# Q, K and V projections in pairs by way of DRAM, and attention woven from three streams

## The chip, the cores and the metric

The kernel runs on one core of a Trainium2 chip. Its time is the device time of one execution in microseconds (us). TensorE (PE) multiplies matrices, VectorE (DVE) and ScalarE (ACT) work elementwise, GpSimd (POOL) does small elementwise work and issues DMAs, SyncE (SP) issues most DMAs. Each engine runs its own instructions in a fixed order and waits for the others by semaphores.

## The reference

One decoder layer for a prompt of 512 tokens and 8 samples of 8 tokens each, 576 tokens in all (`T`), everything in float32. One combined projection of the normalised input (2048 wide) gives z, xBC, dt, q, k, v and three sets of gates; an SSD (scan) branch and a sliding-window attention branch follow, are gated, merged and projected out.

```python
h = _rmsnorm(x, norm_w)
u = jnp.einsum('bld,de->ble', h, w_in)
...
q, k, v, g_attn, mix_s, mix_a = ...        # columns of u; 32 query heads, 8 kv heads of 64
o = _banded_window_attention(q, k, v, rel_table, attn_sinks)   # prompt: window of 128
o = _window_decode_attention(q, kk, vv, rel_table, attn_sinks) # samples: cache of 128 + 8 new
...
s = q.k * scale + bias;  m = max(max(s), sink);  p = exp(s - m)
denom = sum(p) + exp(sink - m);  out = (p / denom) v
...
o = o * silu(g_attn);  p_attn = o @ w_attn_branch
merged = sigmoid(mix_s) * p_ssm + sigmoid(mix_a) * p_attn
x = x + merged @ w_out
```

Outputs are the two normalised results, the last keys and values, and the conv and scan states.

## The kernel before

*Products.* A product in float32 is made of three products of float32r parts: the weight tile (1024 x 128) is split into `wh` (ACT, L80) and `wl` (DVE, L81), the activations are kept as `ah` and `al`, and `wh.ah + wh.al + wl.ah` is summed in PSUM. `run_main` does this plainly: an output tile is 128 columns of the weights for all 576 tokens, as two halves of 288, so 16 row blocks x 2 halves x 3 = 96 matmuls of 288 columns (L345). `pairs_of` takes two output tiles, the two halves of the weight rows and the two halves of the tokens as a 2 x 2 block product and makes it with seven products instead of eight (L453, 7 x 8 x 3 = 168 matmuls); the price is sums of weight tiles on DVE (L393) and additions on the way out (L404).

*Stages.* In order of time: normalisation and the first `FIRST` = 6 mix gates, plainly; the **pair stage**, 22 pairs (16 tiles of the attention gate `ga` and `Z_PAIRED` = 28 tiles of z, stored to DRAM by ACT's DMA queue); the **attention stage**, `run_main` over 38 tiles (4 of K, 4 of V, dt, 16 of Q, 13 mix gates); the **scan stage**, `run_main` over 63 tiles (48 of xBC, 4 of z, 11 mix gates); then the output products, mostly in pairs, and the final normalisation.

*Weaving.* Other work is written as generators in two lists, `quick` and `jobs`. `run_main` calls `pump()` after every six matmuls; each call advances the head of `quick` by one step and `jobs` by `pace["rate"]`/8 steps. So the program's order puts attention and scan between the matmuls. From this order a scheduler makes each engine's list by a simulated timeline: work that would wait lets later work pass. What is wrapped in `keep_in_program_order` does not move on its engine.

*Attention.* `take_q` splits a Q tile straight from PSUM; when the fourth tile of a group of two kv heads is done, `attn_job(m)` is queued. For each of four blocks of 128 queries it makes the scores of 8 heads (L606), adds the bias and takes the maximum (L610), the exponential (L622), divides (L629), transposes (L639), copies (L641), multiplies by the values (L649, 512 columns) and copies into `oT` (L654). `sample_attn` does the same for the 8 samples; its last product is 16 matmuls of 64 columns (L742, L743). Then `oT` is multiplied by the gate on POOL (L665) and stored. The four groups run one after the other. The bias rows come from DRAM (`bias_d`), written during the pair stage by `bias_job` with 16 DMAs of POOL (L491).

*Gates.* A mix gate is a Sigmoid on ACT straight from PSUM (L1127), stored by SP. Where L1127 and the Exp of L622 alternate, the trace has an ACT_TABLE_LOAD ahead of each (11 and 10 of them in the attention stage).

Of the kernel before, what the change touches and what calls it, by code (L numbers as in the profile page):

```python
# [16 lines left out]
P = 128  # L17
D = 2048
# [26 lines left out]
N_A = 40  # L45
# [3 lines left out]
MIXES = (2, 2, 3, 6)  # L49
# [4 lines left out]
Z_PAIRED = 28  # L54
# [31 lines left out]
def hybrid(ctx, tc, x_prompt, x_sample, cache_k, cache_v, state_conv, state_ssm, norm_w, w_in, conv_w,  # L86
# [23 lines left out]

    def scratch(shape, name):
        return dram.tile(shape, F32, tag=name, name=name)
# [9 lines left out]
    ga_d = scratch([D, T], "ga_d")  # L122
    xb_d = scratch([D // 2, TH], "xb_d")
# [18 lines left out]
    eps = pers_tile([P, 1], "eps")  # L142
    sinkb = pers_tile([P, HEADS], "sinkb")
# [10 lines left out]
    vec.memset(eps, EPS)  # L154
    for hf in range(2):
        pl = slice(64 * hf, 64 * hf + 64)
        vec.tensor_copy(two[pl], ident[pl, pl])
# [110 lines left out]
    def open_pools(attention):  # L268
        stk = now["stack"] = ExitStack()
        if attention:  # L270
            cp = kp = stk.enter_context(tc.tile_pool(name="ap", bufs=N_A))
# [6 lines left out]
        now["c"], now["k"], now["kt"] = cp, kp, "c" if attention else "k"  # L278
# [4 lines left out]
    def kten(shape, name="k", dt=F32):  # L283
        return now["k"].tile(shape, dt, tag=now["kt"], name=name)
# [31 lines left out]
    def run_main(tiles, had=(), raws={}, then=None):  # L316
# [33 lines left out]

        n = 0
        while n < len(flat):
# [5 lines left out]
            for only in ((1,), (0,)) if had and n == 0 else ((0, 1),):  # L358
# [112 lines left out]
    def bias_job():  # L471

        rb, parts_ = ev.tile([P, TH], F32, tag="e", name="rb"), []
# [15 lines left out]
        for h in range(0, HEADS, 2):  # L489
            yield from wait(56)  # L490
            tc.keep_in_program_order(pool.dma_start(  # L491
# [3 lines left out]
    kT, vnat = [None] * 4, []  # L495

    def take_k(i):
        def f(ps):
            kT[i] = cten("kT")
            act.activation(sq(kT[i]), ps[:, :, :TH], AF.Copy)  # L500
            quick.append(knat_job(i))
        return f

    kn = {}

    def knat_job(i):
        yield
        if i == 0:
            kn["p"] = kten([P, 512], "knp")
            kn["s"] = kten([P, 512], "kns")  # L510
        p1 = bank()
        ten.transpose(p1[:, 0:P], kT[i][:, 384:512], ident)
        ten.transpose(p1[:NS, P:2 * P], kT[i][:, 512:T], ident)
        act.activation(kn["p"][:, i * P:(i + 1) * P], p1[:, 0:P], AF.Copy)
        act.activation(kn["s"][:NS, i * P:(i + 1) * P], p1[:NS, P:2 * P], AF.Copy)
        yield
        if i == 3:
            store_kv(k_prompt, k_sample, cache_k, kn["p"], kn["s"])
            yield

    def store_kv(out_p, out_s, cache, tp, ts):
        sync.dma_start(out=out_p[0, 0].rearrange("t h d -> t (h d)"), in_=tp)
        for b in range(NB):
            sync.dma_start(out=out_s[0, b, 120:128].rearrange("t h d -> t (h d)"), in_=ts[8 * b:8 * b + 8])
        quick.append(copy_job(out_s, cache))

    def copy_job(out_s, cache):
        for b in range(0, NB, 2):
            tc.keep_in_program_order(pool.dma_start(
                out=out_s[0, b:b + 2, 0:120].rearrange("b t h d -> b (t h d)"),  # L530
                in_=cache[0, b:b + 2, 8:128].rearrange("b t h d -> b (t h d)")))
            yield from wait(12)

    def take_v(i):
        def f(ps):
            vt = cten("vT")
            act.activation(sq(vt), ps[:, :, :TH], AF.Copy)
            quick.append(v_job(i, vt))
        return f

    def v_job(i, vt):
        yield
        if i == 0:
            vnat.extend(kten([P, 512], f"v{b}") for b in range(5))
        p1, p2 = bank(), bank()
        for b in range(4):
            ten.transpose(p1[:, b * P:(b + 1) * P], vt[:, b * P:(b + 1) * P], ident)
        ten.transpose(p2[:NS, :P], vt[:, 512:T], ident)
        for b in range(4):
            (act.activation(vnat[b][:, i * P:(i + 1) * P], p1[:, b * P:(b + 1) * P], AF.Copy) if b % 2 else  # L550
             vec.tensor_copy(vnat[b][:, i * P:(i + 1) * P], p1[:, b * P:(b + 1) * P]))
        act.activation(vnat[4][:NS, i * P:(i + 1) * P], p2[:NS, :P], AF.Copy)
        yield
        if i == 3:
            store_kv(v_prompt, v_sample, cache_v, vnat[3], vnat[4])
            yield

    qT, q_s = {}, {}

    def take_q(m, t):  # L560

        def f(ps):
            for u in range(2):
                qs = qT[m, 2 * t + u] = cten("qs", F32R)
                me, other = slice(64 * u, 64 * u + 64), slice(64 - 64 * u, 128 - 64 * u)
                act.activation(sq(qs)[me], ps[me, :, :TH], AF.Copy, scale=0.125)
                vec.scalar_tensor_tensor(out=sq(qs)[other], in0=ps[me, :, :TH], scalar=0.125, in1=sq(qs)[me],
                                         op0=ALU.mult, op1=ALU.subtract)
            q0 = q_s[m, t] = now["s"].tile([P, NS], F32, tag="qs", name="q0", bufs=8)
            act.activation(q0, ps[:, 1, 512 - TH:TH], AF.Copy, scale=0.125)  # L570
            if t == 3:
                jobs.append(attn_job(m))
        return f

    def attn_job(m):
        oT = [cten("oT") for _ in range(4)]
        bm = []
        for j in range(4):
            b_ = kten([P, 2, 256], "bm")
            sync.dma_start(out=b_, in_=AP(bias_d, (8 * m + 2 * j) * P * BL + 127, [[382, P], [P * BL, 2], [1, 256]]))  # L580
            bm.append(b_)

        ks = []
        for hf in range(2):
            kh, kl = (kten([P, 512], n, F32R) for n in ("kh", "kl"))
            src = kT[m][64 * hf:64 * hf + 64, :512]
            for d in (hf, 1 - hf):
                act.activation(kh[64 * d:64 * d + 64], src, AF.Copy)
            for d in range(2):
                vec.tensor_tensor(out=kl[64 * d:64 * d + 64], in0=src, in1=kh[64 * hf:64 * hf + 64],  # L590
                                  op=ALU.subtract)
            ks.append((kh, kl))
        yield from wait(4)

        def scores(blk):
            lo = 128 if blk == 0 else 0
            mx = stat(8, "mx")
            sc = []
            for j in range(4):
                ps = bank([P, 2, 256])  # L600
                s_ = kten([P, 2, 256], "sc")
                sc.append(s_)
                for i in range(2):
                    h = 2 * j + i
                    for d in range(2):
                        ten.matmul(ps[:, i, lo:256], qT[m, h][:, blk * P:(blk + 1) * P],  # L606
                                   ks[h // 4][d][:, blk * P - 128 + lo:blk * P + P], start=d == 0, stop=d == 1)
# [6 lines left out]
            nm, es, sm = stat(8, "nm"), stat(8, "es"), stat(8, "sm")  # L614
            sk_ = sinkb[:, 8 * m:8 * m + 8]
# [4 lines left out]
            for h in range(8):  # L620
# [3 lines left out]
            yield from wait(3)  # L624
            vec.tensor_tensor(out=sm, in0=sm, in1=es, op=ALU.add)
            vec.reciprocal(sm, sm)
            for h in range(8):
# [3 lines left out]
            yield from wait(6)  # L631
            pts = {}
            kbs = [1] if blk == 0 else [0, 1]
            for hf in range(2):
                for kb in kbs:
                    pt = bank()
                    for r in range(4):
                        j, i = divmod(4 * hf + r, 2)
                        ten.transpose(pt[:, r * P:(r + 1) * P], sc[j][:, i, kb * P:(kb + 1) * P], ident)  # L639
                    ptt = kten([P, 512], "pT")  # L640
                    act.activation(ptt, pt, AF.Copy)  # L641
                    pts[hf, kb] = ptt
                    yield
            yield from wait(2)
            po = bank()
            for kb in kbs:
                for hf in range(2):
                    col = (2 * m + hf) * 64
                    ten.matmul(po[64 * hf:64 * hf + 64, :], vnat[blk - 1 + kb][:, col:col + 64], pts[hf, kb],  # L649
                               start=kb == kbs[0], stop=kb == 1)  # L650
                yield
            for h in range(8):
                hf, r = divmod(h, 4)
                act.activation(oT[h // 2][64 * (h % 2):64 * (h % 2) + 64, blk * P:(blk + 1) * P],  # L654
# [895 lines left out]
```

## Time and profile before

| | |
|---|---|
| median of 3 runs | 3225.19 us (3222.79 to 3232.87) |
| profiled execution, own time | 3228.93 us |
| its span, first to last instruction | 3226.8 us |
| mean granted TensorE clock | 0.983 |
| busy: PE / DVE / ACT / POOL | 3112.4 / 1996.5 / 1473.7 / 482.5 us |
| HBM read / written | 385.79 / 91.81 MB |

In a row of the stage view stand the stretch (us from the span's start), its length, then for each engine its busy time and (x) the instructions in it, then the granted TensorE clock (1.00 is full), the mean busy share of the 16 DMA engines and GB/s. With one line chosen, only that line's matmuls and weight loads are counted. A row of the groups by line has the line, engine, operation, output <- inputs, shape and count, then busy time and mean ns of one, then idle time before them and who ended it. A row of the waits reads: who waited for whom, us in total, times, longest.

### The profile page before, as it was taken

Reading aid. Unit: us, or ns where it says so; the run is one execution under the profiler, and the core shown is the slowest. Engines: PE = TensorE matmul, PEld = TensorE weight load, DVE = VectorE, ACT = ScalarE, POOL = GpSimd, SP = SyncE. Lnnn points to the kernel's source line nnn. Section 1 sums busy time; section 2 is a strip of 40 time slices with the busy share of each in tenths; the row PEclk is TensorE's granted clock in tenths of the full one; section 3 lists DMA queues with packets and bytes.
Section 4 is the critical chain, followed back from the end, with each engine's and each line's share of the span. In section 5 each row is a group of like instructions: output and inputs, shape, how many; then the busy total and the mean of one; then the engine's idle time right before and its main releaser. Section 6 shows DMA issues by size and latency. Waiting matters only on the chain. (4 is left out here: it accounts for less than half of the span.)

```text
span 3226.8 us, 58215 instructions
## 1 busy us (share of the span) xinstructions
PE 3112.4 (96%) x22939; PEld 2993.4 (93%) x22939; DVE 1996.5 (62%) x3434; ACT 1473.7 (46%) x2761; POOL 482.5 (15%) x591
## 2 busy tenths in 40 slices
PE   6989999999999999999999999999999999999997
PEld 5989999999898998999999999998899989998997
DVE  6656666515444443477687687686657777877354
ACT  5434444423554554455555555565433433434333
POOL 3200000000001010112213212212221031311111
PEclk9999999999999999999999999999999999999999
DMA  6564444433343243364464564565575676967655
GB/s 198 143 156 121 122 123 125 117 89 90 84 121 93 82 123 100 100 165 135 135 179 128 147 166 132 148 166 146 147 234 175 194 212 143 249 159 194 180 161 158
DMA packets 733650, 471.18 MB, mean 146 GB/s; under 512 B 45433, under 2 KB 696969, under 8 KB 733185
## 3 DMA queue, kind: packets, MB, share of 16 engines
q1 hardware_dynamic: 691616, 420.51, 46.6%
q0 software_dynamic: 24336, 29.20, 4.4%
q10 hardware_dynamic: 17424, 17.76, 1.7%
q8 instruction: 180, 2.95, 0.4%
q14 instruction: 94, 0.76, 0.1%
HBM read 385.79 MB, written 91.81 MB: 148 GB/s over the span
## 5 line engine op out<-in xcount | busy, mean ns | idle before, releaser
L80 ACT ACTIVATE wh<-raw 128x1024 fp32r<-128x1024 f32 x586 | 620.1, 1058 | 1031.6 <-PE ps L453 488.4
L81 DVE TENSOR_TENSOR wl<-raw,wh 128x1024 fp32r<-128x1024 f32 x586 | 728.0, 1243 | 529.9 <-ACT wh L80 525.9
L345 PE MATMUL ps<-ah,wh 128*128 128x288 f32 (+2 forms) x4384 | 1021.4, 302 | 34.8 <-ACT craw L828 10.1
L345 PE MATMUL ps<-ah,wl 128*128 128x288 f32 (+2 forms) x4384 | 1012.6, 301 | 3.5 <-DVE wl L81 3.3
L345 PE MATMUL ps<-al,wh 128*128 128x288 f32 (+2 forms) x4384 | 1012.4, 300 | 2.5 <-DVE al L1170 2.5
L345 PEld LDWEIGHTS ps<-ah,wh 128*128 128x128 f32 x4384 | 735.2, 192 | 50.5 <-issue 11.1
L345 PEld LDWEIGHTS ps<-ah,wl 128*128 128x128 f32 x4384 | 734.5, 191 | 19.6 <-issue 10.6
L345 PEld LDWEIGHTS ps<-al,wh 128*128 128x128 f32 x4384 | 734.6, 191 | 9.0 <-DVE al L1170 4.1
L453 PE MATMUL ps<-ah,wh 128*128 128x288 f32 x1280 | 382.2, 299 | 13.8 <-DVE w L404 5.6
L453 PE MATMUL ps<-ah,wl 128*128 128x288 f32 x1280 | 383.5, 300 | 5.9 <-DVE wl L81 5.4
L453 PE MATMUL ps<-al,wh 128*128 128x288 f32 x1280 | 381.8, 298 | 0.0
L453 PEld LDWEIGHTS ps<-ah,wh 128*128 128x128 f32 x1280 | 244.4, 191 | 14.7 <-issue 5.8
L393 DVE TENSOR_TENSOR raw<-raw 128x1024 f32<-128x1024 f32 x160 | 194.8, 1220 | 97.6 <-DMA raw<-in_w_in_dram 40.6
L453 PEld LDWEIGHTS ps<-ah,wl 128*128 128x128 f32 x1280 | 244.6, 191 | 9.3 <-DVE wl L81 9.2
L453 PEld LDWEIGHTS ps<-al,wh 128*128 128x128 f32 x1280 | 244.7, 191 | 0.1
L844 DVE SCALAR_TENSOR_TENSOR cacc<-craw,prm,cacc 128x600 f32<-128x600 f32 x144 | 126.8, 885 | 45.4 <-ACT cacc L842 43.7
L882 ACT ACTIVATE L<-L,nacs_n 128x128 f32<-128x128 f32 (+1 forms) x320 | 96.7, 379 | 56.6 <-DVE L L879 56.1
L610 DVE CUSTOM_DVE_ANT_0 sc<-bank,bm 128x256 f32<-128x256 f32 (+1 forms) x128 | 43.8, 388 | 80.0 <-PE bank L606 72.1
L923 POOL TENSOR_TENSOR xl<-xe,xh 128x512 fp32r<-128x512 f32 x32 | 58.6, 1832 | 200.3 <-ACT xh L922 199.9
L879 DVE TENSOR_TENSOR L<-L,nacs_n 128x512 f32<-128x512 f32 (+1 forms) x80 | 51.9, 662 | 47.7 <-DMA L<-nacs_d 47.3
L1093 DVE SCALAR_TENSOR_TENSOR s<-s,dec_s,bank 128x128 f32<-128x128 f32 x256 | 70.4, 340 | 10.3 <-PE bank L1087 9.3
L1241 POOL DMA_DIRECT2D dska<-in_d_skip_dram x1 | 0.6, 586 | 455.9 <-DMA z_d<-c 455.9
(575 smaller groups left out, 4497.7 us busy)
## 6 DMA issues: line engine op xcount, KB each, us to landing
raw<-in_w_in_dram SPq DMA_DIRECT2D x306, 512.0 KB
raw<-in_w_ssm_branch_dram SPq DMA_DIRECT2D x64, 512.0 KB
raw<-in_w_out_dram SPq DMA_DIRECT2D x64, 512.0 KB
L<-nacs_d SPq DMA_DIRECT2D x64, 256.0 KB
s<-in_state_ssm_dram SPq DMA_DIRECT2D x64, 256.0 KB
out_dram<-s SPq DMA_DIRECT2D x64, 256.0 KB
raw<-in_w_attn_branch_dram SPq DMA_DIRECT2D x32, 512.0 KB
stg<-y_d SPq DMA_DIRECT2D x48, 288.0 KB
```

Of the source, the lines that this page charges most:

```text
L80: pin(nc.scalar.activation(wh, raw, AF.Copy))
L81: pin(nc.vector.tensor_tensor(out=wl, in0=raw, in1=wh, op=ALU.subtract))
L345: ten.matmul(sums[i][:, s, :part.shape[1]], a[:, kk, :], part, start=(k == 0 and q == 0), stop=(k == last and q == 2))
L393: vec.tensor_tensor(out=s_[x], in0=s_[a], in1=s_[b], op=op)
L453: ten.matmul(st[p]["ps", i][:, :TH], a[:, k, :], b, start=i < 4 and k == 0 and q == 0, stop=k == 7 and q == 2, skip_group_check=i >= 4)
L610: vec.tensor_tensor_reduce(out=s_[:, i, lo:256], in0=ps[:, i, lo:256], in1=bm[j][:, i, lo:256], scale=1.0, scalar=-3e38, op0=ALU.add, op1= ...
L844: vec.scalar_tensor_tensor(out=acc[:, :600], in0=raw[:, i:i + 600], scalar=prm[:, i * 48 + j:i * 48 + j + 1], in1=acc[:, :600], op0=ALU.mu ...
L879: vec.tensor_tensor(out=l_[:rows, :, :n], in0=l_[:rows, :, :n], in1=nacs_n[:rows, blk, h:h + 4].unsqueeze(2).to_broadcast([rows, 4, n]), o ...
L882: act.activation(l_[:rows, i, :n], l_[:rows, i, :n], AF.Exp, scale=-1.0, bias=nacs_n[:rows, blk, h + i:h + i + 1])
L923: pool.tensor_tensor(out=xl, in0=xe, in1=xh, op=ALU.subtract)
L1093: vec.scalar_tensor_tensor(out=sts[i][:, t, :], in0=sts[i][:, t, :], scalar=dec_s[:, 4 * g + t, b:b + 1], in1=ps[:, v, i, :], op0=ALU.mult ...
L1241: pool.dma_start(out=dska, in_=AP(d_skip, 0, [[0, P], [1, H]]))
```

## The change

1. K, V and Q leave the attention stage: `cols` now begins with K, V and Q (12 pairs), stored by ACT to new DRAM buffers `k_d`, `v_d` and `q_d`. `Z_PAIRED` falls from 28 to 24, so the pair stage has 32 pairs. The four other z tiles go to the scan stage, which also takes dt as its first tile and 7 mix gates instead of 11.
2. The attention stage is `run_main` over 17 mix gates with `halves=True`: the two halves of 288 tokens have a PSUM bank each and are taken separately (three banks go round), and `pump()` is called after every six matmuls. Its rate is 15 eighths.
3. `attn_job` is replaced by `attn_jobs`: `weave` runs three generators by due times, `kv_stream(0)` and `kv_stream(1)` (the even and the odd kv heads, four of each, the second 12.4 steps later) and `sample_stream`. A kv head loads its q, k and bias from DRAM by SP, splits them, and handles four heads per block; o is multiplied by the gate on DVE straight out of PSUM (in a bank of its own, `px`) and stored by POOL, which also loads the gate, 128 tokens at a time. The value product is two matmuls of 256 columns. The samples are handled four at a time, so that the last product is 8 matmuls at a time; their caches, queries and gates are loaded by POOL.
4. The gates of this stage are 0.5 + 0.5 tanh(x/2): a Tanh and an Identity on ACT per half, stored by ACT; `take_gate` stores by ACT too.
5. The 16 writes of `bias_d` are issued by ACT, one per 96 steps (before: POOL, one per 56). The loads of the sinks move from the attention stage into `bias_job`.
6. Pools: four separate pools for attention instead of one of 40 buffers.

```diff
-N_A = 40
+N_AC, N_AQ, N_AK, N_AH = 3, 4, 30, 14
-MIXES = (2, 2, 3, 6)
+MIXES = 17
+RATE_A = 15
-Z_PAIRED = 28
+Z_PAIRED = 24
...
+        def by_half(n):
+            i, c = flat[n]
...
+            for s in range(2):
+                if c == 0:
+                    sums[i, s] = pm.tile([P, 512], F32, tag="ps", name="ps")
+                for kk in range(8):
+                    ah, al = (x[s] for x in pairs[c * 8 + kk])
+                    for q, (a, b) in enumerate(((wh, ah), (wh, al), (wl, ah))):
+                        ten.matmul(sums[i, s][:, :TH], a[:, kk, :], b, ...)
+                    if kk % 2:
+                        pump()
+                if c == last:
+                    take(s, sums.pop((i, s))[:, :TH])
...
         for h in range(0, HEADS, 2):
-            yield from wait(56)
-            tc.keep_in_program_order(pool.dma_start(
+            yield from wait(96)
+            tc.keep_in_program_order(act.dma_start(
                 out=AP(bias_d, h * P * BL, [[P * BL, 2], [BL, P], [1, BL]]),
                 in_=AP(oh_d, h * BL, [[BL, 2], [0, P], [1, BL]])))
...
+    def weave(streams):
+        due = [[at, i, gen, step] for i, (gen, at, step) in enumerate(streams)]
+        while due:
+            e = min(due, key=lambda e: e[:2])
+            try:
+                next(e[2])
+            except StopIteration:
+                due.remove(e)
+                continue
+            e[0] += e[3]
+            yield
...
+    def qk_loads(g):
+        qr = [now["q"].tile([P, 512], F32, tag="q", name="qr") for _ in range(2)]
+        for t in range(2):
+            sync.dma_start(out=qr[t][:, :512], in_=q_d[(2 * g + t) * P:(2 * g + t + 1) * P, :512])
...
+    def kv_head(m, hf):
...
+        for blk in range(4):
+            if blk == 3 and m < 3:
+                qk_loads(g + 2)
...
+            ga = hten("ga", [P, 2, P])
+            pool.dma_start(out=ga, in_=AP(ga_d, 2 * g * P * T + blk * P, [[T, P], [P * T, 2], [1, P]]))
+            yield
...
+            po = xbank([P, 2, P])
             for kb in kbs:
-                for hf in range(2):
-                    ten.matmul(po[64 * hf:64 * hf + 64, :], vnat[blk - 1 + kb][:, col:col + 64], pts[hf, kb], ...)
+                for u in range(2):
+                    ten.matmul(po[64 * u:64 * u + 64], vn[:, blk - 1 + kb, 64 * hf:64 * hf + 64],
+                               pts[kb][:, u::2, :], start=kb == kbs[0], stop=kb == 1)
+            o_ = hten(f"o{"AB"[hf]}", [P, 2, P])
+            vec.tensor_tensor(out=o_, in0=po, in1=ga, op=ALU.mult)
+            pool.dma_start(out=AP(o_d, 2 * g * P * T + blk * P, [[T, P], [P * T, 2], [1, P]]), in_=o_)
...
+    def attn_jobs():
+        yield from weave([(kv_stream(0), 0, 1.0), (kv_stream(1), 12.4, 1.0), (sample_stream(), 5, 1.65)])
...
+    def take_half(dst, n):
+        def f(s, ps):
+            t_ = now["c"].tile([P, TH], F32, tag="e", name="mix")
+            act.activation(t_, ps, AF.Tanh, scale=0.5)
+            act.activation(t_, t_, AF.Identity, bias=half, scale=0.5)
+            act.dma_start(out=dst[n * P:(n + 1) * P, s * TH:(s + 1) * TH], in_=t_)
+        return f
...
-    for off, dst, m in ((OFF_GA, ga_d, D // P), (0, z_d, Z_PAIRED)):
+    for off, dst, m, func in ((OFF_K, k_d, KVW // P, AF.Copy), (OFF_V, v_d, KVW // P, AF.Copy),
+                              (OFF_Q, q_d, D // P, AF.Copy), (OFF_GA, ga_d, D // P, AF.Silu),
+                              (0, z_d, Z_PAIRED, AF.Silu)):
...
-    pace["rate"] = 9
-    run_main(seq)
+    jobs.append(attn_jobs())
+    pace["rate"] = RATE_A
+    run_main([m_in(c, take_half(d_, n)) for c, d_, n in mixes[FIRST:FIRST + MIXES]], halves=True)
     drain()
...
-    seq = []
+    seq = [m_in(OFF_DT, take_dt)]
```

More of the change, by code (lines that the diff above doesn't have):

```diff
@@ L521, in store_kv @@
[L521 to L573, printed above, removed]
@@ L697, in sample_attn @@
         ss = []
-        for i in range(4):
+        for i in range(2):
             ps = bank()
@@ L1266, in hybrid @@
     open_pools(False)
+    pace["rate"] = 9
+    ms.close()
+    ms = ExitStack()
+    pm = ms.enter_context(tc.tile_pool(name="pm", bufs=2, space=PSUM, reuse_waits="tile"))
     def last_x(g):
```

368 lines of the change are left out of this document (197 added, 171 removed).

## The prediction

> **What bounds the kernel now.** I read the page's busy shares first, then the busy time by stage, then what TensorE waits for in each stage, then its clock.
>
> ```profile
> PE 3112.4 (96%) x22939; PEld 2993.4 (93%) x22939; DVE 1996.5 (62%) x3434; ACT 1473.7 (46%) x2761; POOL 482.5 (15%) x591
> core 0: us, PE busy (x) PEld busy (x) DVE busy (x) ACT busy (x) POOL busy (x), PEclk, DMA share, GB/s
> 122.70:629.20 506.50, 497.01 (x3707) 495.07 (x3706) 331.94 (x358) 205.27 (x275) 18.55 (x19) 0.99 0.49 130
> 629.20:1285.50 656.30, 654.55 (x4691) 605.29 (x4690) 266.70 (x756) 303.34 (x717) 32.96 (x69) 0.98 0.35 99
> 1285.50:2334.50 1049.00, 1025.37 (x7779) 977.26 (x7778) 733.78 (x1277) 562.85 (x1161) 236.59 (x260) 0.99 0.54 145
> ```
>
> The three rows are the pair stage (22 pairs), the attention stage (38 tiles) and the scan stage (63 tiles). TensorE is busy 98% to 99.7% of each; no other engine passes 70%. So time is TensorE's instructions times their spacing, plus its waits, plus the time at a low clock. The spacing of a 288-column matmul is the same in both kinds of stage when nothing disturbs it:
>
> ```profile
> 220.00:320.00 100.00, 100.00 (x758) 100.00 (x757) 1.00 0.45 125
> 700.00:800.00 100.00, 98.42 (x743) 97.34 (x743) 1.00 0.33 88
> 629.20:1285.50 656.30, 534.28 (x3736) 507.46 (x3735) 0.98 0.35 99
> ```
>
> First row: the pair line L453 alone, 100/758 = 131.9 ns. Second: the plain line L345, 98.42/743 = 132.5 ns. A plain tile is 96 matmuls, 12.72 us; a pair of tiles is 168 instead of 192, 22.16 us instead of 25.44. The third row is L345 over the whole attention stage: 143 ns of busy union each, so something slows this stage.
>
> **The change, part by part.**
>
> *Products.* K, V and Q (24 tiles) leave the plain loop and become 12 pairs; 4 z tiles go from 2 pairs back to it. Plain: 38 + 63 tiles become 17 + 64 (dt moves to the head of the scan stage), so 20 x 12.72 = 254.4 us go. Pairs: 10 more, 221.6 us come. The rest of a pair's work is hidden: the pair stage needs 331.94/22 = 15.1 us of DVE and 9.3 us of ACT per 22.16 us. Writing q, k and v through ACT and reloading them is hidden by the same margin, and by a DMA share of 0.49 and 0.35. **-32.8 us.**
>
> *Clock.* Here is the low clock of the attention stage, with what ran just before:
>
> ```profile
> 172.20:175.60 3.40, 3.40 (x15) 3.40 (x16) 2.26 (x3) 1.51 (x2) 0.00 (x0) 0.51 0.74 207
> 192.70:202.90 10.20, 6.82 (x27) 6.50 (x28) 7.94 (x9) 2.35 (x4) 0.00 (x0) 0.50 0.30 82
> 923.20:930.00 6.80, 6.80 (x30) 6.35 (x29) 2.80 (x16) 0.00 (x0) 4.05 (x3) 0.50 0.17 67
> 1039.20:1046.00 6.80, 6.80 (x25) 6.10 (x26) 2.97 (x9) 2.53 (x3) 2.46 (x2) 0.50 0.00 0
> 1162.10:1168.90 6.80, 6.80 (x27) 6.43 (x27) 3.00 (x9) 1.06 (x1) 4.15 (x3) 0.50 0.14 47
> 1285.00:1288.40 3.40, 3.40 (x15) 3.40 (x15) 2.47 (x9) 1.06 (x1) 2.65 (x2) 0.50 0.10 40
> 919.80:923.20 3.40, 2.00 (x10) 1.32 (x10) 1.00 0.00 0
> 919.80:923.20 3.40, 0.00 (x0) 0.00 (x0) 1.00 0.00 0
> 967.60:971.00 3.40, 0.06 (x1) 0.00 (x0) 1.00 0.32 93
> ```
>
> The clock is granted in steps of 3.4 us, and the last four low stretches each follow one cluster of `sample_attn`'s 64-column output matmuls (L742, L743; seventh row: L743 alone, ten in 3.4 us; eighth: L345 in that stretch, none). A stretch equally empty of L345 but full of 256- and 512-column attention matmuls (last row) is followed by full clock. So it is the narrow cluster that trips it: 16 matmuls in a row fill a whole step. Its price is 23.8 us at half clock, 11.9 us lost. The change cuts each cluster into two of 8 with other work between: half a step each. I take all four as gone, **-11.9 us**; the other end is that each of the eight trips one step of 3.4 us, 8 x 1.7 = 13.6 us, +1.7.
>
> The Trainium skill ("TensorE: Matmul & The Clock Gate", section "HAM oscillation — how this bites in real kernels") asks only for no idle gaps above about 3.4 us. Here the profile shows TensorE busy ahead of those drops, so the rows differ from it; by the rule alone this term would be nothing and the sum 12 us later.
>
> *Bias writes.* The first two low-clock rows lie in the pair stage. There the 16 writes of the bias table crowd together, though the code spreads them by 56 steps each, because POOL has nothing else to do:
>
> ```profile
> L491 POOL DMA_DIRECT2D bias_d<-oh_d x16: 1054/1061/1116, 137.1 to 176.3; - x16
> DMA to landing us min/median/max: 15.4/22.0/25.9
> 160.00:180.00 20.00, 17.43 (x118) 16.97 (x117) 11.66 (x12) 6.62 (x11) 7.39 (x7) 0.91 1.01 223
> 180.00:200.00 20.00, 13.08 (x85) 12.54 (x84) 8.43 (x10) 4.52 (x6) 0.00 (x0) 0.82 0.71 157
> DVE raw L393 <- DMA raw<-in_w_in_dram: 18.1, 3, 11.1
> PE ps L453 <- DVE w L404: 5.6, 1, 5.6
> L1138 ACTq DMA_DIRECT2D z_d<-c x28: 326/326/327, 337.7 to 630.5; - x28
> ```
>
> The DMA engines are full, DVE waits 18.1 us for weights, TensorE idles 2.57 + 6.92 = 9.5 us, and its busy 3.40 + 6.82 us at half clock lose 5.1. The change issues them from ACT, held in order among ACT's own work, one per 96 steps (96 x 3 x 131.9 ns = 38 us). ACT pays an issue each; its other stores take 0.33 us (last row), hidden in an engine 41% busy. If ACT blocks on one as long as the POOL instruction lasts, 1.1 us, that is hidden too. **-14.6 us**, of which I take -14 for what a single write may still hold up; the other end is 0, if they still bunch.
>
> *Attention woven.* In the old stage the 3736 plain matmuls take 3736 x 0.1325 = 495 us, the low clock 11.9, waits 1.8; so attention and dt leave 656.3 - 508.7, near 148 us of TensorE. This work stays but for the probability-value products: 112 of 512 columns become 224 of 256.
>
> ```profile
> L649 PE MATMUL bank<-pT,v 128*64 128x512 f32 x112 | 47.3, 618 | 0.0
> L606 PE MATMUL bank<-kh,qs 128*128 128x256 f32 (+1 forms) x128 | 34.2, 292 | 0.0
> PE ps L345 <- ACT q L570: 1.8, 1, 1.8
> PE ps L345 <- ACT craw L828: 10.1, 4, 3.2
> L622 ACT ACTIVATE sc<-sc,nm 128x256 f32<-128x256 f32 (+1 forms) x128 | 59.9, 469 | 8.9 <-DVE nm L617 8.8
> L622 ACT ACTIVATION_READ_ACCUMULATOR sc<-sc,nm 128x1 f32 x128 | 23.9, 187 | 0.0
> L80 ACT ACTIVATE wh<-raw 128x1024 fp32r<-128x1024 f32 x78 | 82.6, 1058 | 177.0 <-PE ps L345 138.9 <-issue 34.6 <-DMA raw<-in_w_in_dram 2.2
> L654 ACT ACTIVATE oT<-bank 64x128 f32<-64x128 f32 x128 | 34.7, 271 | 53.9 <-PE bank L649 52.5
> ```
>
> A product of 512 columns costs 47.3/112 = 0.42 us, one of 256 columns 0.27 (34.2/128); so 224 cost between half of 0.42 and 0.27 each, 47 to 60 us: 0 to +13; I take **+4**, near the first since they run back to back. The new stage is 17 x 12.72 + 148 + 4 = 368 us. ACT loses the copies of oT (34.7), the q0 copies and its table loads, and gains a second pass per gate half (34 x about 0.4); with 34 splits instead of 78 it has near 245 us, DVE near 210. Neither is full, but nearer to it than before, and the chain of a block (scores, maximum, exp, scale, transpose, copy, product) has less between its links. The old stage waited 1.8 us; the scan stage, as mixed, waits 23.6 of 1049 (its largest row is 10.1). For 368 us that makes 8 us by the scan stage's rate. I take **+8** (1.8 to 16, twice the rate). At RATE_A = 15 the 388 steps of the three streams are given out in some 210 of the 272 pumps; 3.8 plain tiles, 48 us, cover what comes late. dt at the head of the scan stage delays nothing: its first reader, the first group's scan, starts seven tiles later. PSUM is handed over twice instead of once: **+1.5**.
>
> Sum: -32.8 - 11.9 - 14 + 4 + 8 + 1.5 = -45.2. The profiled execution took 3228.9 us by its own time (span 3226.8), so 3183.7; that execution stands 3.7 us above the median of 3225.2, from which the sum would give 3180. I say 3184.
>
> **The rivals.** What a measurement of this kernel can tell from no change is about 0.3%, 9.7 us.
>
> *Bias writes stay bunched* (ACT lets them through early, or ACT is held up by them): the step doesn't do what it says, and the time is 3184 + 14 = 3198. For it: marking them as ordered didn't spread them on POOL. Against: ACT has work on both sides of each. 0.13.
>
> *The dense stage starves.* A link of the softmax comes late and TensorE, in order, stands. At 10% of the 300 us in which attention is given out it costs 30 instead of 8: 3206; at 16%, 3224. For it: 148 us of other work beside some 165 us of tiles, against 495 before. Against: the 1.8 us row. 0.15.
>
> *POOL becomes the bound (slower).* The change puts 120 DMAs on POOL's queue in this stage: 64 loads of ga and stores of o (two for each of 32 blocks) and 56 of the k, v, cache and sample rows; POOL's other work there falls to about 15 us.
>
> ```profile
> L1350 POOL DMA_DIRECT2D mg_d<-o x27: 841/855/949, 2595.8 to 2947.2; - x27
> L667 SPq DMA_DIRECT2D o_d<-oT x16: 319/332/653, 927.4 to 1292.3; - x16
> 629.20:1264.50 635.30, 520.40 (x3645) 494.85 (x3644) 0.98 0.36 100
> ```
>
> At 0.59 (L1241 below) to 1.06 us (L491) each that is 71 to 127 us: hidden. The old stage's last plain tile ended at 1264.5 (38 tiles are 3648 matmuls; second row: L345 alone, 3645 up to there) and its last store of o was issued at 1292.3 (first row), so the scan stage's tiles hid 28 us of overhang. To cost anything, an issue must take (368 + 28 - 15)/120 = 3.2 us; from 3.55 us on it eats the whole gain, and at 3.7 us the kernel takes about 3247. 0.03. The Trainium skill's "SBUF — State Buffer", section "SBUF: two separate sides", speaks for this rival: a DMA issued from POOL waits for its descriptors while DVE holds the shared port, and it gives 3.1 us in place of 0.62. This trace doesn't agree so far: L1350 takes 0.86 us beside a DVE 74% busy.
>
> *The clock falls in the dense stage (slower).* If every 3.4 us step with little main work tripped, a third of its 90 steps, it would lose 30 x 1.7 = 51 us and take about 3235. The same skill page on the clock says ("Part 4: PE-mode transpose") that transposes do not count as busy, which speaks for it. The 967.6 row speaks against. 0.05.
>
> **How the numbers follow.** As forecast 0.60, its own range 3171 (every term at its good end) to 3201 (products and waits at their dear ends); bunched 0.13; starved 0.15 (a third of it under 9.7 us of gain); POOL 0.03; clock 0.05; better than 3164 (a gain that I don't see) 0.04. The range 3164 to 3212 leaves out that 0.04, the two slower ones and half of the starved. Faster 0.60 + 0.13 + 0.10 + 0.04 = 0.87, same 0.05, slower 0.08.
>
> **What would show it.** The pair stage grows to 32 pairs and about 506.5 + 222 - 14 = 714 us, without its hole at 168 to 195 us; the bias writes start some 38 us apart. The attention stage takes 350 to 375 us with no step of half clock behind a narrow cluster, and TensorE waits there under 16 us. The first loads of attention still stand until the pair stage's last stores land, as this one does:
>
> ```profile
> L1241 POOL DMA_DIRECT2D dska<-in_d_skip_dram x1: 586/586/586, 633.3 to 633.3; - x1
> ```
>
> It is wrong if TensorE shows waits on the softmax of tens of us, if POOL is idle nowhere in that stage, if the low clock appears among wide attention matmuls, or if the last store of o comes more than 28 us after the stage's last tile.

## The result, and the profile after

The changed kernel takes **3187.17 us** (median of 4 runs, 3183.47 to 3190.59) against 3223.99 for the one before: a ratio of 0.9880, 95% interval 0.9866 to 0.9894. The forecast was 3184 (3164 to 3212). The profiled execution took 3184.28 us, its span is 3182.4, its granted clock 0.986.

The sum came out, but not by its terms: of the three large ones only the products delivered what was written down, and the rest netted to about the forecast for other reasons than those given.

The stage view of after: start, pair stage, attention stage, scan stage (here up to the first output pair), output pairs, end. Before, cut at the matching instants (122.7, 628.6, 1264.4, 2434.2, 2972.1), the lengths were 122.7, 505.9, 635.8, 1169.8, 537.9 and 254.7 us.

```profile
0.00:131.40 131.40, 100.18 (x660) 93.21 (x661) 89.32 (x209) 63.22 (x135) 33.91 (x44) 0.97 0.54 162
131.40:862.20 730.80, 718.39 (x5382) 715.45 (x5381) 481.04 (x517) 296.51 (x394) 3.74 (x7) 1.00 0.46 128
862.20:1235.80 373.60, 363.52 (x2686) 328.75 (x2684) 218.60 (x887) 200.79 (x553) 90.98 (x170) 0.97 0.49 138
1235.80:2401.30 1165.50, 1144.71 (x8681) 1095.63 (x8680) 820.24 (x1384) 604.33 (x1231) 247.86 (x288) 0.99 0.55 152
2401.30:2932.40 531.10, 513.21 (x3792) 509.15 (x3793) 398.64 (x533) 206.55 (x272) 105.34 (x135) 0.99 0.70 185
2932.40:3182.40 250.00, 223.77 (x1618) 217.34 (x1616) 116.50 (x224) 94.50 (x142) 31.18 (x35) 0.96 0.59 179
```

Length by length: start +8.7, pair stage +224.9, attention -262.2, scan -4.3 (though dt and its 12.7 us came into it, and before it still held the old attention's overhang), output pairs -6.8, end -4.7; together -44.4. The last two stages have the same matmuls as before and a little less time at a low clock; nothing in them was changed.

What TensorE waited for in the pair stage (first two rows), what DVE waited for there (after, then before), and what TensorE waited for in the attention stage:

```profile
PE ps L491 <- DVE wl L82: 7.7, 5, 1.7
PE ps L491 <- DVE w L442: 4.7, 3, 1.7
DVE raw L431 <- DMA raw<-in_w_in_dram: 65.8, 31, 7.2
DVE raw L393 <- DMA raw<-in_w_in_dram: 37.5, 22, 11.1
PE bank L679 <- DVE scB L668: 4.2, 2, 4.0
PE bank L561 <- DMA vT<-v_d: 3.4, 1, 3.4
PE bank L686 <- ACT pTB L681: 0.9, 2, 0.5
PE bank L782 <- DVE pw L777: 0.9, 1, 0.9
PE bank L563 <- DMA kq<-k_d: 0.6, 1, 0.6
```

The one hole of 10 us in the old pair stage has become eight short waits behind five writes, 12.4 us together, and DVE stands longer for weights than before. In the attention stage TensorE waits 10.0 us.

### The profile page after: what moved, and what is told of

Read it like the earlier page. It is cut to its first block, busy times and chain, and to the rows that moved or that the text cites. A ratio compares the mean times of both kernels' runs of the same rounds, so it can differ in the third digit from the quotient of the medians.

```text
span 3182.4 us, 58573 instructions
## 1 busy us (share of the span) xinstructions
PE 3063.8 (96%) x22811; PEld 2959.5 (93%) x22811; DVE 2124.3 (67%) x3751; ACT 1465.9 (46%) x2723; POOL 513.0 (16%) x679
## 5 line engine op out<-in xcount | busy, mean ns | idle before, releaser
L82 DVE TENSOR_TENSOR wl<-raw,wh 128x1024 fp32r<-128x1024 f32 x616 | 765.6, 1244 | 430.7 <-ACT wh L81 429.0
L363 PE MATMUL ps<-ah,wh 128*128 128x288 f32 (+2 forms) x3200 | 753.1, 301 | 22.7 <-ACT craw L869 6.4
L363 PE MATMUL ps<-al,wh 128*128 128x288 f32 (+2 forms) x3200 | 754.5, 300 | 3.4 <-DVE al L1217 3.4
L363 PE MATMUL ps<-ah,wl 128*128 128x288 f32 (+2 forms) x3200 | 748.8, 300 | 4.0 <-DVE wl L82 3.9
L363 PEld LDWEIGHTS ps<-ah,wh 128*128 128x128 f32 x3200 | 538.8, 191 | 30.5 <-ACT craw L869 6.6
L363 PEld LDWEIGHTS ps<-ah,wl 128*128 128x128 f32 x3200 | 539.5, 191 | 10.6 <-DVE wl L82 6.9
L491 PE MATMUL ps<-ah,wh 128*128 128x288 f32 x1600 | 474.7, 297 | 14.7 <-ACT ah L1216 6.3
L491 PE MATMUL ps<-ah,wl 128*128 128x288 f32 x1600 | 475.9, 297 | 10.4 <-DVE wl L82 10.3
L491 PE MATMUL ps<-al,wh 128*128 128x288 f32 x1600 | 474.2, 296 | 0.0
L431 DVE TENSOR_TENSOR raw<-raw 128x1024 f32<-128x1024 f32 x200 | 243.6, 1220 | 124.9 <-DMA raw<-in_w_in_dram 68.8
L491 PEld LDWEIGHTS ps<-ah,wh 128*128 128x128 f32 x1600 | 302.9, 189 | 16.1 <-ACT ah L1216 6.7
L491 PEld LDWEIGHTS ps<-ah,wl 128*128 128x128 f32 x1600 | 303.0, 189 | 13.5 <-DVE wl L82 13.4
L491 PEld LDWEIGHTS ps<-al,wh 128*128 128x128 f32 x1600 | 303.0, 189 | 0.1
L380 PE MATMUL ps<-ah,wh 128*128 128x288 f32 x544 | 164.8, 303 | 0.0
L380 PE MATMUL ps<-al,wh 128*128 128x288 f32 x544 | 164.5, 302 | 0.0
L380 PE MATMUL ps<-ah,wl 128*128 128x288 f32 x544 | 163.9, 301 | 0.0
L380 PEld LDWEIGHTS ps<-al,wh 128*128 128x128 f32 x544 | 104.8, 193 | 2.4 <-issue 2.3
```

The lines of the kernel that those rows point to most:

```text
L82: pin(nc.vector.tensor_tensor(out=wl, in0=raw, in1=wh, op=ALU.subtract))
L363: ten.matmul(sums[i][:, s, :part.shape[1]], a[:, kk, :], part, start=(k == 0 and q == 0), stop=(k == last and q == 2))
L380: ten.matmul(sums[i, s][:, :TH], a[:, kk, :], b, start=c == 0 and kk == 0 and q == 0, stop=c == last and kk == 7 and q == 2)
L431: vec.tensor_tensor(out=s_[x], in0=s_[a], in1=s_[b], op=op)
L491: ten.matmul(st[p]["ps", i][:, :TH], a[:, k, :], b, start=i < 4 and k == 0 and q == 0, stop=k == 7 and q == 2, skip_group_check=i >= 4)
```

## The experiments

Theory at the outset: the products carry the gain, and the weave of attention gives nothing. Rival: the weave carries part of it. The other runs each take one term of the sum by itself. The kernel before, run beside them, took 3222.49 to 3225.95 us.

**K, V and Q made plainly again**, ahead of the pair stage; the bias writes then go out every 56 steps instead of 96, so that they end with the shorter pair stage:

```diff
-            yield from wait(96)
+            yield from wait(56)
...
-    for off, dst, m, func in ((OFF_K, k_d, ...), (OFF_V, v_d, ...), (OFF_Q, q_d, ...), (OFF_GA, ga_d, ...),
-                              (0, z_d, Z_PAIRED, AF.Silu)):
+    for off, dst, m, func in ((OFF_GA, ga_d, D // P, AF.Silu), (0, z_d, Z_PAIRED, AF.Silu)):
...
+    plain = [m_in(off + n * P, by_halves(gate_out(AF.Copy, dst, n))) for off, dst, m in
+             ((OFF_K, k_d, KVW // P), (OFF_V, v_d, KVW // P), (OFF_Q, q_d, D // P)) for n in range(m)]
```

> K, V and Q of the changed kernel are made by the plain loop ahead of the pair stage instead of in 12 pairs, everything else as changed (the bias writes go out every 56 steps so that they end with the shorter pair stage). Theory (the gain is the saved products): 24 tiles x 12.72 = 305 us come, 12 pairs x 22.16 = 266 us go, so 39 us are given back: about 3226 us, level with the kernel before. Rival (the gain is the weave and its cover, the pairs only moved work): less than 15 us back, about 3200.

3223.96 us, ratio 0.9997 (0.9986 to 1.0008): the gain is gone. Its attention stage (first row) has the length of the changed kernel's to the tenth; the second row is its pair stage, of 20 pairs:

```profile
885.90:1259.50 373.60, 360.79 (x2686) 326.35 (x2685) 219.37 (x887) 200.83 (x553) 90.45 (x170) 0.97 0.49 137
439.50:885.90 446.40, 446.40 (x3367) 445.47 (x3366) 301.26 (x325) 186.68 (x250) 3.73 (x7) 1.00 0.48 136
```

So without these pairs there is no gain left. As a price the 36.8 us between the two kernels are less clean. Up to the end of the pair stage this run is 23.7 us longer, not 39, because its bias writes cost nothing there: TensorE is busy for all of the stage (more below). Another 16.2 us, by the profiled executions, come in the stages behind attention, which the edit doesn't touch. The pace of the pairs is better read from the stage itself, 446.4/20 = 22.3 us each. Nor is the weave shown to be worth nothing: this run makes four z tiles plainly that the kernel before paired, 6.6 us by the prediction's figures, and still equals it, with small gains and losses beside it that it can't tell apart.

**The bias writes.** First, back on POOL:

```diff
-            yield from wait(96)
-            tc.keep_in_program_order(act.dma_start(
+            yield from wait(56)
+            tc.keep_in_program_order(pool.dma_start(
```

> The 16 bias writes go back to POOL, one per 56 steps, everything else as changed. The prediction's step (spreading them by way of ACT saves 14 us): about 3201 us, with a hole of some 9 us near the first bias writes. Rival (each spread write costs about what its share of the burst cost: the changed kernel has eight short waits of 12.4 us in all in its pair stage): within 4 us of the changed kernel, about 3187, one long hole in place of the eight short ones.

3180.79 us, 0.9864 (0.9845 to 0.9882), within noise of the changed kernel. The writes bunch again and make one hole; spread, they make many small ones for the same price (pair stage 728.4 us here, 730.8 spread). The rows of the bias writes, of TensorE's largest wait and of the stage in this run, then the bias writes of the changed kernel:

```profile
L536 POOL DMA_DIRECT2D bias_d<-oh_d x16: 1054/1060/1091, 143.9 to 183.8; - x16
PE ps L491 <- DVE w L442: 8.6, 1, 8.6
131.40:859.80 728.40, 717.34 (x5382) 715.39 (x5382) 482.97 (x518) 294.66 (x392) 21.27 (x24) 0.99 0.48 129
```
```profile
L536 ACTq DMA_DIRECT2D bias_d<-oh_d x16: 600/601/1182, 180.6 to 770.1; - x16
180.60:195.40 14.80, 13.14 (x98) 12.74 (x97) 5.11 (x6) 4.54 (x5) 0.00 (x0) 1.00 0.41 98
```

The last row is the stretch behind the first spread write (180.6): the DMA engines are only 41% busy in the mean, yet DVE waits 7.2 us for a weight tile there. Next, the same bytes as 32 writes of one head each, half the size:

```diff
-        for h in range(0, HEADS, 2):
-            yield from wait(96)
+        for h in range(HEADS):
+            yield from wait(48)
...
-                out=AP(bias_d, h * P * BL, [[P * BL, 2], [BL, P], [1, BL]]),
-                in_=AP(oh_d, h * BL, [[BL, 2], [0, P], [1, BL]])))
+                out=AP(bias_d, h * P * BL, [[BL, P], [1, BL]]),
+                in_=AP(oh_d, h * BL, [[0, P], [1, BL]])))
```

> The bias table is written by 32 DMAs of one head, one per 48 steps, instead of 16 of two heads, one per 96; ACT issues them as before. In the changed kernel 5 of the 16 writes are followed by waits of 1.2 to 1.7 us on late weights, 12.4 us and a low step in all. Theory (a write of 383 KB holds the weight loads back for longer than their slack, one of half the size does not): the waits go, 10 to 14 us saved, about 3175. Rival (it is the bytes that cost, however cut): the same waits in smaller pieces, 3187.

3171.74 us, 0.9837 (0.9819 to 0.9855). The pair stage, its writes, and DVE's wait for weights, halved to no more than 2.2 us at a time:

```profile
126.70:840.00 713.30, 713.30 (x5382) 712.37 (x5381) 482.84 (x517) 296.12 (x394) 3.72 (x7) 1.00 0.48 131
L536 ACTq DMA_DIRECT2D bias_d<-oh_d x32: 477/477/565, 156.7 to 747.9; - x32
DVE raw L431 <- DMA raw<-in_w_in_dram: 32.4, 31, 2.2
```

TensorE is busy for all of it. The same writes in the kernel *before*, 36 steps apart and issued by ACT instead of POOL:

> The kernel before with one part alone: its bias writes issued by ACT, 32 of one head, one per 36 steps. Theory (the burst costs the old pair stage 14.6 us, as the prediction worked out, and small spread writes cost nothing): its hole at 169 to 196 us goes and the time is 3210. Rival (the hole has another cause): 3225.

3206.88 us, 0.9954 (0.9938 to 0.9971); its pair stage (505.9 before) has no wait either:

```profile
120.80:611.50 490.70, 490.70 (x3701) 489.76 (x3701) 331.56 (x357) 205.36 (x274) 1.64 (x3) 1.00 0.49 134
```

So 32 writes of one head cost nothing in either kernel, where 16 of two heads cost 15 to 17.5 us of the pair stage. That the size is what matters isn't shown, for two reasons.

The first is the place. A step is three matmuls of the 168 of a pair, so 56 steps are just one pair: in e1 all 16 writes, of the full 383 KB, go out at the same place, near matmul 73 of a pair, and TensorE never stood. With 96 steps seven places take turns. The five writes with waits behind them are the three near matmul 25 of a pair (180.6, 453.3 and 725.6 us) and the two near matmul 1 (337.2 and 609.6); none of the eleven at the other five places has one. The count of L491 alone up to a write at such a place in the changed kernel (3529 = 21 x 168 + 1), then the same for the third write of e1 (577 = 3 x 168 + 73), and e1's writes:

```profile
131.40:609.62 478.22, 469.53 (x3529) 467.73 (x3530) 1.00 0.47 129
439.50:517.20 77.70, 76.92 (x577) 76.50 (x578) 1.00 0.47 130
L536 ACTq DMA_DIRECT2D bias_d<-oh_d x16: 596/597/1209, 472.8 to 806.5; - x16
```

The second is the shape. By the packets of the traces, a write of two heads from ACT takes 9 to 12 us and keeps fewer than 2.2 of the 16 DMA engines busy; one of a single head is over in 1 to 3.5 us, on several engines at a time. What ACT's queue moved in the 12 us of the first write, then in 3 us of a write of e8 (packets, MB, share of 16 engines):

```profile
q10 hardware_dynamic: 258, 0.39, 9.3%
q10 hardware_dynamic: 122, 0.16, 37.1%
```

So the edit of e8 changed the width of a write along with its size, and a mean of 41% can hide a few engines that are busy throughout. The late tile came at 193.2, about when the write ended; that it waits for its parts on those few engines is likely, but not shown. No run wrote two heads at once over many engines, which would tell size from width.

**The start.** The 8.7 us lost there were no part of the forecast. The eight copies of the old caches to the outputs (480 KB each) lost their ordering mark in the change; the scheduler put them among the very first. The copies before and after, the loads of the prompt before and after (ns min/median/max, then first and last start), and TensorE's wait for the normalised input, before and after:

```profile
L529 POOL DMA_DIRECT2D out_dram<-in_cache_k_dram x4: 539/550/577, 40.9 to 42.6; - x4
L183 SPq DMA_DIRECT2D x<-in_x_prompt_dram x8: 432/528/4319, 2.4 to 16.4; - x8
PE bank L245 <- DVE x L211: 12.7, 6, 6.9
```
```profile
L579 POOL DMA_DIRECT2D out_dram<-in_cache_k_dram x4: 539/540/586, 6.3 to 13.2; - x4
L192 SPq DMA_DIRECT2D x<-in_x_prompt_dram x8: 432/1236/10901, 2.4 to 25.0; - x8
PE bank L254 <- DVE x L220: 18.0, 5, 6.9
```

One issue of SP now takes 10.9 us; in the two runs below, with the copies elsewhere, the slowest takes 3.4 and 3.2. First the mark was put back:

```diff
-            pool.dma_start(out=out[0, 2 * m:2 * m + 2, 0:120].rearrange("b t h d -> b (t h d)"),
+            tc.keep_in_program_order(pool.dma_start(
+                out=out[0, 2 * m:2 * m + 2, 0:120].rearrange("b t h d -> b (t h d)"),
```

> The 8 copies of the k and v caches to the outputs are held in POOL's program order again, so that they leave from the attention stage and not at 6 to 14 us, when the prompt is being loaded. Theory (they cost the start 8.7 us): the first plain matmul starts at 25 us instead of 32, the pair stage at 123 instead of 131, and the time falls by 5 to 9 us, to about 3180. Rival (the first stage is late for another reason): start unchanged. If the 3.8 MB then disturb the attention stage, that stage grows above 374 us.

3195.89 us, 0.9904 (0.9887 to 0.9921): no gain, and rather slower than the changed kernel, though the intervals touch. The start did fall by 15.0 us, but the copies now come in the attention stage (178 POOL instructions instead of 170), which is 13.7 us longer; the pair stage loses 4.4, and the stages behind, which the edit doesn't touch, 8.9:

```profile
0.00:116.40 116.40, 93.76 (x660) 86.87 (x661) 87.79 (x209) 62.78 (x135) 30.51 (x36) 1.00 0.52 149
116.40:851.60 735.20, 722.53 (x5383) 719.58 (x5382) 481.18 (x517) 296.62 (x394) 3.74 (x7) 0.99 0.45 127
851.60:1238.90 387.30, 366.46 (x2685) 330.07 (x2684) 220.61 (x887) 201.65 (x553) 95.01 (x178) 0.96 0.49 143
```

Then the copies went to ACT, as 16 of 240 KB between the bias writes of the pair stage:

```diff
-            yield from wait(96)
+            yield from wait(72)
...
+            yield from wait(24)
+            out, cache, b = ((k_sample, cache_k), (v_sample, cache_v))[(h // 2) % 2] + ((h // 2) // 2,)
+            tc.keep_in_program_order(act.dma_start(out=out[0, b:b + 1, 0:120]..., in_=cache[0, b:b + 1, 8:128]...))
```

> Only the cache copies are moved: issued by ACT in the pair stage, 16 of 240 KB, each between two bias writes of 383 KB. Theory (they cost the start 15 us because the prompt waits for them, and the pair stage has room: DMA share 0.46): first plain matmul at 24 us, 10 to 15 us saved, about 3175. Rival (a write beside the weights costs the same anywhere): the pair stage grows by what the start gains, 3187.

3182.43 us, 0.9879 (0.9861 to 0.9896). The copies cost the pair stage nothing and the start is 14.7 us shorter (116.7), but attention takes 3.8 us more and the scan stage 7.8:

```profile
116.70:847.00 730.30, 719.13 (x5382) 716.40 (x5381) 481.29 (x517) 296.80 (x394) 3.72 (x7) 0.99 0.47 133
847.00:1224.40 377.40, 364.16 (x2687) 329.36 (x2685) 219.93 (x887) 200.85 (x553) 90.68 (x170) 0.96 0.48 136
1224.40:2397.70 1173.30, 1149.24 (x8681) 1099.27 (x8680) 818.09 (x1384) 604.31 (x1232) 248.07 (x288) 0.99 0.55 151
```

The same scan code takes 1165 to 1173 us among these kernels, so a gain of 15 us at the start can be half lost in a stage that nothing touched. Why it falls as it does in each stays open.

**The tail of the attention stage.** The forecast said that the last tiles would cover what comes late. They didn't; the plain line of this stage (L380) alone, and the longest of the waits behind its end:

```profile
862.20:1213.40 351.20, 241.65 (x1632) 225.64 (x1632) 0.98 0.51 142
1222.25 0.45 PE L679 MATMUL bank<-ident,scB 128*128 128x128 f32 x2 [4.04 <-DVE scB L668]
```

All 17 x 96 = 1632 matmuls are done by 1213.4, and attention runs alone until 1235.8, 22 us with its links in the open. Is it given out too slowly, or held by its own chain? Rate 15 to 24:

> Attention is given out at 24 eighths of a step per call instead of 15, so its 388 steps are over after 130 of 272 calls in the program's order instead of 210. In the changed kernel the last plain matmul of the stage ends at 1213.4 us and attention goes on alone to 1235.8. Theory A (attention runs late because its chains and buffers hold it, not because it is given out late): the tail stays, 15 to 25 us, and the time is 3187 +/- 5, or longer if TensorE waits more. Theory B (given out too slowly): the tail is gone and 8 to 11 us are saved, about 3178.

3192.74 us, 0.9897 (0.9873 to 0.9921): the stage takes 377.8 us and the tail stays (the 1632 matmuls are done by 1220, the stage ends at 1241). Giving it out faster doesn't help. More tiles beside it, `MIXES` 17 to 19 (two mix gates fewer in the scan stage):

> Two more gate tiles (25 us of plain matmuls) stand in the attention stage and two fewer in the scan stage, so TensorE's work is the same. In the changed kernel TensorE idles 6.3 us in the 22 us tail and runs 10 us of it at half clock. Theory (the tail is uncovered for want of plain tiles): the tail's waits and its two low steps go, 8 to 11 us saved, about 3178. Rival (the tail moves along, since attention is held back by the plain tiles that it stands among): no change, 3187.

3182.04 us, 0.9878 (0.9852 to 0.9904). Two tiles are 25.4 us, and the stage grows by 17.1, the scan stage shrinks by 22.8:

```profile
860.30:1251.00 390.70, 385.46 (x2878) 351.48 (x2877) 223.78 (x892) 206.76 (x562) 93.01 (x173) 0.98 0.49 138
1251.00:2393.70 1142.70, 1119.04 (x8490) 1069.32 (x8488) 815.95 (x1379) 601.92 (x1229) 250.43 (x285) 0.99 0.55 153
```

TensorE waits little to its end now, and the span is 4.9 us shorter; the interval of the ratio doesn't separate it from the changed kernel.

**The narrow clusters** were cut once more, into four and four products:

```diff
+            if b == 1:
+                yield from wait(2)
```

> The samples' last product is given out as 4 + 4 narrow matmuls with two steps between them instead of 8 in a row. In the changed kernel four of the eight clusters end in a step of half clock (922, 1014, 1059 and 1233 us, 17 us in all, 8.5 us lost). Theory (a step of 3.4 us nearly without wide matmuls trips the clock): the low steps behind the clusters fall to at most one, 5 to 8 us saved, about 3180. Rival (the scheduler puts the halves together again, or other attention work fills the step in the same way): as many low steps, 3187.

3186.55 us, 0.9881 (0.9856 to 0.9906). Half-clock steps behind clusters fall from four to two; but in e6, whose clusters are not cut again, there are two as well (1055.6 and 1236.5), so the fall can't be put down to this edit. The attention stage is 14.7 us shorter, with no wait at its end, and the scan stage 14.5 longer: the last samples' work (37 matmuls) passed into it, and TensorE stood 9.2 us more there.

**Tanh gates.** A Sigmoid again, which alternates with the Exp:

```diff
-            act.activation(t_, ps, AF.Tanh, scale=0.5)
-            act.activation(t_, t_, AF.Identity, bias=half, scale=0.5)
+            act.activation(t_, ps, AF.Sigmoid)
```

> The gates of the attention stage are one Sigmoid pass each instead of Tanh and Identity. ACT saves 34 passes of about 0.4 us and gets table loads of 1.28 us again, up to two for each gate half. Theory (ACT, busy 201 of 374 us, is not the bound): within 4 us of the changed kernel, 3187. Rival (the softmax chain is short of time, so that each table load holds up TensorE): 20 to 50 loads x 1.28 us longer by 10 to 40 us, 3200 to 3230.

3190.57 us, 0.9891 (0.9874 to 0.9909): no difference clear of noise. The table loads come back, 66.7 us of them in three groups, and ACT is busy 252 us of a stage of 367.8, with room for them:

```profile
L1176 ACT ACT_TABLE_LOAD x26 | 33.4, 1283 | 0.5
L661 ACT ACT_TABLE_LOAD x22 | 28.2, 1283 | 4.8 <-ACT mix L1176 3.1 <-DMA ms_d<-mix 1.3 <-ACT vn L570 0.2
862.20:1230.00 367.80, 360.20 (x2695) 325.57 (x2693) 219.82 (x890) 252.03 (x571) 92.45 (x170) 0.98 0.50 142
```

**Together:** fine bias writes, the copies on ACT in the pair stage, 19 tiles, and v loaded ahead of q and k:

> The changed kernel with what the runs so far point to: bias writes of one head, 48 steps apart (measured: 15 us saved); the 8 cache copies taken out of the attention code and issued by ACT as 16 of one sample and 240 KB between the bias writes (the start alone was 15 us earlier when they left it); 19 gate tiles in the attention stage (5 us saved); v loaded ahead of q and k for each pair of heads (the wait of 3.4 us for it and the low step behind it). If the parts add up: 3187 - 15 - 10 - 5 - 5 = 3152. If the copies only move their cost into the pair stage, as they did into the attention stage: 3165.

**3157.06 us**, 0.9797 (0.9782 to 0.9811). The gains nearly add up; start (117.4) and pair stage keep theirs:

```profile
117.40:830.80 713.40, 713.40 (x5383) 712.46 (x5382) 482.88 (x517) 296.19 (x394) 3.74 (x7) 1.00 0.50 136
```

Loading v first did nothing: the wait of 3.4 us for it at the head of attention stays at 3.35.

## Why the prediction was right, step by step

- **Products, -32.8: right.** The pair stage at its own pace is 713.3 us (e8), where 714 was forecast: 22.3 us a pair, in e1 as in e8. Without the pairs for K, V and Q the time is back at 3224, though e1 alone doesn't give the size of this term.
- **Clock, -11.9: failed, about 0.** The attention stage has 27.2 us at half clock. The four stretches in the prediction were 23.8; with one it left out (3.4 us from 885.9) the old stage had 27.2 too. Two of the new ones stand behind idle time (3.4 us for v at 871, 4.04 at 1218). Four stand behind narrow clusters. L782 alone in the step ahead of one of these; all lines in the step behind it; then L380 alone in three steps, the first that same one, the others with clusters that don't trip the clock:

```profile
918.80:922.20 3.40, 1.70 (x8) 1.15 (x8) 1.00 0.85 233
922.20:925.60 3.40, 3.40 (x17) 3.40 (x16) 3.25 (x23) 0.63 (x2) 0.00 (x0) 0.50 0.35 107
918.80:922.20 3.40, 0.00 (x0) 0.00 (x0) 1.00 0.85 233
1103.00:1106.40 3.40, 0.93 (x7) 0.69 (x6) 1.00 0.47 151
1195.10:1198.50 3.40, 0.46 (x3) 0.49 (x4) 1.00 0.46 137
```

The step that failed is "16 matmuls in a row fill a whole step. ... half a step each". In the trace each of these products is two records, eight of L782 in the first row and as many of L781: a halved cluster still takes some 2.8 of the 3.4 us (918.3 to 921.1). In the changed kernel the four clusters with at most one plain matmul in their step trip, the four with three or more don't; but in e7 steps with 6 and 7 plain matmuls tripped too, so no count of them draws the line. "TensorE: Matmul & The Clock Gate" of the Trainium skill (section "HAM oscillation — how this bites in real kernels") names idle gaps alone; that agrees with the two behind idle time and not with these four.
- **Bias writes, -14: failed as made, about 0; the amount was right.** They were spread some 38 us apart as said and the hole went. What failed is that "what a single write may still hold up" was put near nothing: behind five of the 16 TensorE stood 1.2 to 3.3 us, 12.4 together, and behind one of them came 6.8 us at half clock. It is the price of the rival "bias writes stay bunched" by a mechanism that it didn't name: a write of two heads holds TensorE up when it falls at two of the seven places in a pair. e1, e8 and e11, without any such wait, show the 15 us to be there for the taking.
- **Value products, +4: sign wrong, -11.5 by the same rows.** 224 of 256 columns take 18.3 + 17.5 = 35.8 us against 47.3, 0.16 each, under the lower end of 0.21. (These are records of the trace, two for each product.) No run tried why, but the timelines give a hint. Before, two records in a row took 1.07 us (26 times) and four in a row 1.08 (10 times), so a second product, into the other half of the partitions, added next to nothing when it came right behind the first; more often it didn't. Now four mostly stand together, 0.65 us for four (35 times). The step that failed is the lower bound: half of 0.42, which is a mean over both kinds, was no floor:

```profile
L686 PE MATMUL bank<-pTB,vn 128*64 128x256 f32 x112 | 18.3, 419 | 0.9 <-ACT pTB L681 0.9
L686 PE MATMUL bank<-pTA,vn 128*64 128x256 f32 x112 | 17.5, 402 | 0.1
```

- **Waits, +8: right (10.0),** but they aren't the links in the dense part: 7.4 of the 10 are the first load of v and one wait in the tail. The starving rival did not come: softmax links cost 6.0 us, tail included.
- **Cover of 48 us of tiles: wrong.** The tiles ended at 1213.4, and attention had 22 us to go. Its last store of o (1236.7, second row below) comes 23 us after the last tile, inside the 28 that the forecast allowed: that mark was set too loosely to show the failure.
- **POOL: right.** 91 us busy of 373.6, and its stores cost 0.71 us. The 3.1 us that the Trainium skill ("SBUF — State Buffer", section "SBUF: two separate sides") gives for a DMA issued from POOL beside a DVE copy doesn't appear here, with a DVE 59% busy:

```profile
L690 POOL DMA_DIRECT2D o_d<-oA x16: 706/711/727, 902.6 to 1219.0; - x16
L690 POOL DMA_DIRECT2D o_d<-oB x16: 706/712/725, 928.6 to 1236.7; - x16
```

- **Missing: the start, +8.7.** The diff took an ordering mark off eight DMAs, and the forecast didn't ask where they would go.

The 26 us of clock and bias that did not come, and the start's 8.7, were made up by the value products (near 16 better than written) and by the stages behind: scan, output pairs and end are 15.8 us shorter, though dt's 12.7 came in. Part of that is the old attention's overhang, which the scan stage no longer holds; the rest was not tested. So the total was met partly by luck: errors that cancel.

## What to carry to other kernels

Spreading big DRAM writes in time does not by itself free a weight stream: where each falls in the loop decides what it costs. Give them a period of one loop body at a harmless place (e1), or cut them so that each is small and runs on many engines (e8). Look at the longest wait for weights and at what each queue does, not at the mean share of the DMA engines. When a diff drops an ordering mark from a DMA that depends on nothing, ask where the scheduler will put it, and move it to a stage with slack, not merely back. Give a stage of woven work enough dense tiles to outlast its longest chain: a faster rate doesn't shorten the chain.

## What was not expected of the hardware

- A DRAM-to-DRAM write of 383 KB from ACT kept about 1.5 of 16 DMA engines busy for some 11 us (0.39 MB at 9.3% of 16 over 12 us) and delayed a weight load by up to 7.2 us; by its place in the pair TensorE stood for up to 3.3 us behind it or not at all. With writes of 191.5 KB, each over in 1 to 3.5 us, the longest wait was 2.2 us and TensorE never stood.
- ACT's issue of such a write took 0.60 us at 383 KB and 0.48 at 191.5 KB.
- Eight copies of 480 KB issued at 6 to 14 us stretched one issue of SP, of prompt loads, to 10.9 us; the slowest before was 4.3.
- A record of a value product of 256 columns cost 0.16 us, one of 512 columns 0.42; four records of 512 columns in a row took no longer than two (1.08 and 1.07 us).
